# Paired weight jobs of a one-core decoder layer: the weight sums move to SBUF-to-SBUF transfers, more slots for raw weights

## The chip, the cores and the metric

The kernel runs on one core of a Trainium2 chip. The time is what the device takes for one execution, in microseconds (us). Three runs of the kernel before gave 1238.41, 1242.54 and 1246.62 us; the median, 1242.54, is its time.

## The reference

One decoder layer for a prompt of 512 tokens and a sample group of 8 x 4 tokens, 544 columns in all, d_model 1024, in float32:

```
x = x + 0.5 * SwiGLU_1(RMSNorm(x))                  # d_ff 2816
z = RMSNorm(x) @ w_in                               # 28 column blocks of 128
x = x + concat(MoBA(q_a, k_a, v_a), gate * norm(HGRN2(q_b, f_b, i_b))) @ w_out
x = x + 0.5 * SwiGLU_2(RMSNorm(x))
swiglu(x) = (silu(x @ w_gate) * (x @ w_up)) @ w_down
```

MoBA is a block-sparse attention with 8 heads of 64 (the sample group reads a paged cache of 1024 tokens through a page table), HGRN2 a gated linear recurrence with 4 heads of 128. Outputs are both groups' activations, the new keys and values and the recurrent states.

## The kernel before, in words

**Number format.** Every product of weights and activations is done in three float32r matmuls. A weight tile is split into a high part (ScalarE copies it to float32r) and a low part (VectorE subtracts the high part from the raw tile); so are activations. `products` (L667) then adds hi*hi, hi*lo and lo*hi into PSUM, 272 columns (half of 544) at a time.

**Units and jobs.** A weight unit is a raw tile of 128 rows by up to 4 blocks of 128 columns and its two parts (`split_unit`, L593). `weight_jobs` (L502) lists the jobs in the order of use. A plain job has two units for one column block. A paired job computes a 2 x 2 arrangement of blocks with seven products instead of eight (a Strassen-Winograd form): seven units, made of the quarters a11, a12, a21, a22 and of sums of them. For gate and up it takes one feature block f of both matrices, with units of 4 blocks (256 KB each) and 7 x 4 x 3 = 84 matmuls, where the two plain jobs have 96. For down it takes two output blocks, with 192 KB or 128 KB units. In each FFN the feature blocks 0 to `NREG` - 1 are plain, the others and all of down are paired. The 22 feature blocks go in groups of 6, 6, 4 and 6; after each group comes its part of down.

**Loading and splitting.** `w_load` (L575) issues one raw block per call: a plain load on SP's queue and, where the entry names a second source, an accumulating transfer of it from HBM on POOL's queue. A paired job loads five blocks, (a21 + a22), (a11 + a21), a11, a12, a22. `w_split` (L600) begins a paired job when all five have been issued; at unit 0 VectorE makes two more sums into separate tiles S0 and S1, and all seven units follow. `room` (L544) hands out slots: 6 raw and 4 split-unit slots, and in stretches of the FFNs more of both, made from tiles that are free there (`more_slots`, L560). `w_pump` (L631) splits up to `AHEAD` = 4 units ahead and loads as long as there are raw slots.

**Factors.** A paired job also needs the activations in paired form. `right_factors` (L720) makes them for gate and up in 4 sets of 18 steps on VectorE and ScalarE, spaced by `PACE`; `raw_hidden` and `hidden_paired` make the hidden ones for down.

**Order.** Nothing is scheduled on the chip. A planner (`Order`) runs through the whole program as coroutines, a backbone of matmuls and side chains, with a price for every instruction and transfer (`Engine.call`, `Order.dma` at L360), and sorts each stretch by the modelled start. The five engines then execute their queues in that order; an instruction that waits holds up all that stand behind it on its engine. All instructions are recorded at one line (L286), so the trace tells them apart by tile names: `raw`, `S`, `whi`, `wlo` for weights, `xw` for factors, `hw` for hidden factors, `xh`, `xl` for activations, which also serve as extra raw and split-unit slots, `mm` and `sm` for PSUM. `small` (L962) loads small constants and builds a table of relative biases through DRAM (`rbias`, then `rprompt` and `rsample`) during the first FFN. In the mixer (`project`, `mix`) the 28 input projections are plain jobs, between attention, recurrence and gathers of the cache that POOL issues.

Of the kernel before, what the change touches and what calls it, by code (L numbers as in the profile page):

```python
# [21 lines left out]
KD = D // 128  # L22
# [30 lines left out]
NREG = 6  # L53
AHEAD = 4
PACE = 0.8
# [124 lines left out]
class Engine:  # L180
# [75 lines left out]
class Order:  # L256
# [158 lines left out]
class Factors:  # L415
# [4 lines left out]
    def __init__(self, build, home, raw):  # L420
        self.nc = build.nc
        self.t = [build.tl(home(i)[0], [128, 2, HT], home(i)[1], F32R) for i in range(7)]
        self.u = [build.tl(raw[0], [128, 2, HT], t) for t in raw[1:]]
# [39 lines left out]
class Build:  # L463
# [38 lines left out]
    def weight_jobs(self):  # L502
# [14 lines left out]
        def plain(m, nk, r0, c0):  # L517
            job(None, [(q,) for q in quarters(m, nk, r0, c0)], nk)

        def paired(kind, nk, a11, a12, a21, a22):  # L520
            job(kind, [(a21, a22), (a11, a21), (a11,), (a12,), (a22,)], nk)
# [17 lines left out]
        for m in range(KD):  # L539
            plain(a["w_out"][0], KD, 0, 128 * m)  # L540
# [34 lines left out]
    def w_load(self):  # L575
# [10 lines left out]
        for more in src[1:]:  # L586
            self.nc.gpsimd.dma_start(raw_k, more, accum_op=ALU.add)
# [5 lines left out]
    def split_unit(self, src, nk, x):  # L593
        nc = self.nc
        hi, lo = self.take_slot(x, (F32R, F32R))
        nc.scalar.copy(hi[:, :nk], src[:, :nk])
        nc.vector.tensor_tensor(lo[:, :nk], src[:, :nk], hi[:, :nk].bitcast(F32), op=ALU.subtract)
        return hi, lo, x

    def w_split(self):  # L600
# [4 lines left out]
        if len(job["raw"]) <= (4 if job["paired"] else n) or (job["paired"] and len(self.xw) < KD // 2):  # L605
            return False
        x = self.room("w", job)
        if x is None:
            return False
        nk = job["nk"]  # L610
# [109 lines left out]
    def right_factors(self, pool, x, gain):  # L720
# [5 lines left out]
        for k in range(n):  # L726
            f = Factors(self, lambda i: (pool, f"xw{7 * k + i}"), (pool, "S0", "S1"))
# [4 lines left out]
            for step in steps + f.first() + f.right() + f.left():  # L732
                step()
# [80 lines left out]
    def raw_hidden(self, i, hs):  # L814
# [3 lines left out]
        if not odd:  # L818
            hs.append(Factors(self, lambda k: self.hidden_home(7 * p + k), (self.sums, "U0", "U1")))
# [142 lines left out]
    def small(self, rp):  # L962

        nc, a = self.nc, self.a
        loads = []

# [4 lines left out]
        self.lmi = rp.tile([128, 5, 16], I32, name="lmi")  # L971
# [21 lines left out]
        self.tab = rp.tile([33, HEADS], F32, name="tab")  # L993
# [929 lines left out]
```

## Time and profile before

| | |
|---|---|
| median of 3 runs | 1242.54 us (1238.41 to 1246.62) |
| the profiled execution | 1247.47 us, span 1245.7 us |
| TensorE / VectorE / ScalarE / POOL busy | 94% / 79% / 50% / 23% of the span |
| mean granted TensorE clock | 0.982 |
| read from HBM | 176.41 MB |
| first FFN, mixer with w_out, second FFN (about) | 17 to 437, 437 to 866, 866 to 1241 us |

Busy times are unions of the instructions' records; matmuls are pipelined, so a single record (about 290 ns) is longer than the distance between two of them. PE is TensorE, PEld its weight load, DVE VectorE, ACT ScalarE, POOL GpSimd, SP the engine that only issues transfers. In the timeline the bracket gives the idle time just before an instruction and what ended it.

### The profile page before, as it was taken

To read this page: it belongs to the slowest core of one execution; us is meant where nothing else is said; L and a number is where in the kernel's file an instruction comes from. 1 tells how busy PE (TensorE), PEld (TensorE's weight loads), DVE (VectorE), ACT (ScalarE), POOL (GpSimd) and SP (SyncE) were. 2 spreads that over 40 slices of the span, in tenths; PEclk is the share of its full clock that TensorE was granted. 3 is DMA by queue.
4 is the path that set the end of the run, shared out by engine and by line. 5 is a ranking of instruction groups with operands and counts; after the bars stand their busy time and mean duration, and the time that the engine had idled before them with its cause. 6 is when DMAs were issued, how large, how long until landed. Compare 5 with 4: busy or idle time off the path is not lost.

```text
span 1245.7 us, 27096 instructions
## 1 busy us (share of the span) xinstructions
PE 1172.4 (94%) x10339; PEld 1096.8 (88%) x10339; DVE 989.0 (79%) x2220; ACT 625.8 (50%) x1345; POOL 289.8 (23%) x271
## 2 busy tenths in 40 slices
PE   9998798999898899999999999899999899998998
PEld 8997797999898898888888877699998899998998
DVE  5998687989787869888768557657987799898896
ACT  5444554465464534555555533344443665555653
POOL 3012212222212240000133333330022222222220
PEclk9999899999998998999999999899999999999999
DMA  6248768885976572322456677452258778959764
GB/s 182 67 96 171 163 129 201 180 164 122 189 147 127 151 227 81 93 81 86 144 155 212 205 233 231 164 157 77 86 129 173 156 151 169 198 106 207 159 141 104
DMA packets 303102, 187.27 MB, mean 150 GB/s; under 512 B 15717, under 2 KB 290972, under 8 KB 302972
## 3 DMA queue, kind: packets, MB, share of 16 engines
q1 hardware_dynamic: 235100, 120.76, 34.2%
q0 software_dynamic: 67776, 64.64, 27.5%
q8 instruction: 81, 1.33, 0.4%
q14 instruction: 49, 0.40, 0.1%
q10 hardware_dynamic: 96, 0.14, 0.0%
HBM read 176.41 MB, written 11.83 MB: 151 GB/s over the span
## 4 chain that ended last, share of the span: by engine, by line
PE 46%; DVE 13%; ACT 3%; issue 2%; DMA 2%; DVEq 0%; POOL 0%; ACTq 0%; POOLq 0%; SPq 0%
PE mm L286 25%; PE sm L286 21%; DVE wlo L286 2%; DVE xl L286 2%; DVE U L286 1%; DVE S L286 1%; DMA raw<-ffn_gate 1%; DVE y L286 1%; DVE sc L286 1%; ACT xl L286 1%; DMA raw<-ffn_up 1%; DVE st L286 1%; ACT xh L286 0%; DVE ms_qk L286 0%; ACT sq L286 0%
## 5 line engine op out<-in xcount | busy, mean ns | idle before, releaser
L286 PE MATMUL mm<-xh,whi 128*128 128x272 f32 x997 | 299.7, 302 | 2.3 <-DVE y L286 2.3
L286 PE MATMUL mm<-xl,whi 128*128 128x272 f32 x998 | 289.0, 291 | 5.3 <-DVE xl L286 4.5
L286 PE MATMUL mm<-xh,wlo 128*128 128x272 f32 x966 | 280.8, 291 | 2.3 <-DVE wlo L286 2.3
L286 ACT CAST whi<-raw 128x512 fp32r<-128x512 f32 (+2 forms) x233 | 134.8, 583 | 147.3 <-PE mm L286 74.0
L286 PEld LDWEIGHTS mm<-xh,whi 128*128 128x128 f32 x997 | 189.4, 190 | 18.3 <-issue 16.9
L286 PEld LDWEIGHTS mm<-xl,whi 128*128 128x128 f32 x998 | 189.8, 190 | 7.7 <-DVE xl L286 6.1
L286 PEld LDWEIGHTS mm<-xh,wlo 128*128 128x128 f32 x966 | 183.9, 190 | 2.9 <-DVE wlo L286 2.8
L286 DVE TENSOR_TENSOR wlo<-raw,whi 128x512 fp32r<-128x512 f32 (+2 forms) x233 | 153.1, 671 | 24.4 <-ACT whi L286 23.6
L286 POOL DMA_DIRECT2D raw<-ffn_down x51 | 64.5, 1286 | 314.2 <-DVE S L286 62.1
L286 PE MATMUL mm<-xw,xh 128*128 128x272 f32 x544 | 103.6, 289 | 2.9 <-DVE U L286 2.9
L286 PE MATMUL sm<-xw,xh 128*128 128x272 f32 x512 | 98.2, 290 | 4.1 <-ACT t_g L286 3.5
L286 PEld LDWEIGHTS mm<-xw,xh 128*128 128x128 f32 x544 | 85.1, 188 | 4.1 <-DVE U L286 3.6
L286 POOL DMA_DIRECT2D raw<-ffn_up x38 | 48.7, 1315 | 159.6 <-DVE U L286 25.3
L286 PEld LDWEIGHTS sm<-xw,xh 128*128 128x128 f32 x512 | 81.2, 191 | 5.1 <-ACT t_g L286 3.7
L286 PE MATMUL mm<-xw,xl 128*128 128x272 f32 x272 | 78.7, 289 | 0.4 <-DVE xl L286 0.2
L286 PE MATMUL sm<-xw,xl 128*128 128x272 f32 x256 | 74.4, 291 | 1.7 <-DVE xl L286 1.7
L286 PE MATMUL sm<-xw,whi 128*128 128x272 f32 x384 | 73.2, 289 | 0.0
L286 PE MATMUL mm<-xw,whi 128*128 128x272 f32 x352 | 68.8, 293 | 0.9 <-DVE U L286 0.9
L286 ACT CAST xh<-raw 128x512 fp32r<-128x512 f32 (+2 forms) x94 | 52.4, 561 | 32.7 <-DMA raw<-ffn_up 18.5
L286 PEld LDWEIGHTS sm<-xw,whi 128*128 128x128 f32 x384 | 60.1, 188 | 0.7 <-issue 0.6
L286 PEld LDWEIGHTS mm<-xw,whi 128*128 128x128 f32 x352 | 56.4, 192 | 2.2 <-DVE U L286 1.4
L286 POOL DMA_INDIRECT KV<-cache_k,idx x32 | 32.8, 1025 | 104.6 <-PE sm L286 63.3
(365 smaller groups left out, 2985.0 us busy)
## 6 DMA issues: line engine op xcount, KB each, us to landing
raw<-ffn_gate SPq DMA_DIRECT2D x90, 256.0 KB
raw<-ffn_down SPq DMA_DIRECT2D x91, 192.0 KB
raw<-ffn_up SPq DMA_DIRECT2D x60, 256.0 KB
raw<-w_in SPq DMA_DIRECT2D x56, 256.0 KB
raw<-ffn_up POOLq DMA_DIRECT2D x38, 256.0 KB
raw<-ffn_down POOLq DMA_DIRECT2D x39, 192.0 KB
xl<-ffn_up POOLq DMA_DIRECT2D x20, 256.0 KB
xh<-ffn_up SPq DMA_DIRECT2D x16, 256.0 KB
```

Source lines behind the costliest of these rows:

```text
L286: call(*map(real, args), **{k: real(v) for k, v in kw.items()})
```

## The change

A paired job's five blocks become a11, (a21 + a11), a22, (a21 + a22), a12, and the added operand is the raw tile that already lies in SBUF. VectorE's two sums go in place, into a11 at unit 1 and into a12 at unit 5. Unit 0 may be split as soon as the first block is issued, units 1 and 2 after the fourth, the rest after the fifth. The low part of a22, made at unit 1 and kept for unit 6, and the low part of the second unit of every plain job but w_out's, no longer come from VectorE: ScalarE writes the negated tile in float32r and an accumulating transfer on POOL's queue adds the raw tile. `NREG` goes from 6 to 5. Raw slots beyond the 6 go from 4 to 10 in the gate/up stretches and from 4 to 12 in the first FFN's last down stretch, split-unit slots from 4 + 6 to 5 + 3 and from 4 + 8 to 5 + 4. The factors use other raw tiles, alternating, and are made two steps at a time every 1.1 us. The planner's prices of transfers change. The first projection of the mixer does both column halves at once. The small constants share a tile of another pool.

```diff
-NREG = 6
+NREG = 5
-PACE = 0.8
+PACE = 1.1
...
+                pool = self.part == "pool"
                 s = self.order.dma(self.part, 4 * args[1].shape[0] * self.free(args[1]), names,
-                                   1.0 if self.part == "pool" else 0.06)
+                                   1.3 if pool else 0.06, 2.5 if "accum_op" in kw else 2.0)
...
-    def dma(self, part, size, names, cost=0.06):
+    def dma(self, part, size, names, cost=0.06, latency=2.0):
         s = self.fit(part, self.start(part, names), cost)
-        e = self.fit("dma", s + cost + 1.5, size / 330e3) + size / 330e3
+        e = self.fit("dma", s + cost + latency, size / 280e3) + size / 280e3
...
         def paired(kind, nk, a11, a12, a21, a22):
-            job(kind, [(a21, a22), (a11, a21), (a11,), (a12,), (a22,)], nk)
+            job(kind, [(a11,), (a21, 0), (a22,), (a21, 2), (a12,)], nk)
...
         self.nc.sync.dma_start(raw_k, src[0])
-        for more in src[1:]:
-            self.nc.gpsimd.dma_start(raw_k, more, accum_op=ALU.add)
+        for n in src[1:]:
+            self.nc.gpsimd.dma_start(raw_k, job["raw"][n][0][:, :job["nk"]], accum_op=ALU.add)
...
-    def split_unit(self, src, nk, x):
+    def split_unit(self, src, nk, x, transfer=False):
+
         nc = self.nc
         hi, lo = self.take_slot(x, (F32R, F32R))
         nc.scalar.copy(hi[:, :nk], src[:, :nk])
+        if transfer:
+            nc.scalar.activation(lo[:, :nk], src[:, :nk], AF.Identity, scale=-1.0)
+            nc.gpsimd.dma_start(lo[:, :nk], src[:, :nk], accum_op=ALU.add)
+            return hi, lo, x
...
-        if len(job["raw"]) <= (4 if job["paired"] else n) or (job["paired"] and len(self.xw) < KD // 2):
+        if len(job["raw"]) <= ((0, 3, 3, 4, 4, 4, 4)[n] if job["paired"] else n):
             return False
...
         if job["paired"]:
-            s1, s3, a11, a12, a22 = (r for r, _ in job["raw"])
-            if n == 0:
-                S = [self.tl(self.sums, [128, 4, 128], f"S{i}") for i in range(2)]
-                for out, p, q in ((S[0], s1, a11), (S[1], a12, S[0])):
-                    self.nc.vector.tensor_tensor(out[:, :nk], p[:, :nk], q[:, :nk], op=ALU.add)
-                job["units"] = (a11, S[0], s1, a12, s3, S[1], a22)
-            self.units.append(self.split_unit(job["units"][n], nk, x))
-            drop = {0: (2,), 2: (0,), 3: (3,), 4: (1,), 6: (4,)}.get(n, ())
+            a11, s3, a22, s1, a12 = (r for r, _ in job["raw"])
+            if n in (1, 5):
+
+                out, p = (a11, s1) if n == 1 else (a12, a11)
+                self.nc.vector.tensor_tensor(out[:, :nk], out[:, :nk], p[:, :nk], op=ALU.add)
+            src = (a11, a11, s1, a12, s3, a12, a22)[n]
+            if n < 6:
+                self.units.append(self.split_unit(src, nk, xs[0]))
+            else:
+                self.units.append(job["last"])
+                self.release(xs[0])
+            if last:
+                job["last"] = self.split_unit(a22, nk, xs[1], True)
+            drop = {1: (2,), 2: (3,), 4: (1,), 5: (0, 4)}.get(n, ())
         else:
-            self.units.append(self.split_unit(job["raw"][n][0], nk, x))
+            self.units.append(self.split_unit(job["raw"][n][0], nk, xs[0], n == 1 and job["transfer"]))
...
-            f = Factors(self, lambda i: (pool, f"xw{7 * k + i}"), (pool, "S0", "S1"))
+            f = Factors(self, lambda i: (pool, f"xw{7 * k + i}"),
+                        [self.hidden_home(14 + k % 2 * 2 + i) for i in range(2)])
...
-            for step in steps + f.first() + f.right() + f.left():
-                step()
+            steps += f.first() + f.right() + f.left()
+            for i in range(0, len(steps), 2):
+                for step in steps[i:i + 2]:
+                    step()
                 self.order.t = self.order.free["pe"] + PACE
                 yield
...
-                        self.more_slots("a", home, [f"{t}{i}" for i in range(2) for t in ("xh", "xl")],
-                                        [(f"xh{i}", f"xl{i}") for i in range(2, KD)])
+                        self.more_slots("a", home, [f"{t}{i}" for i in range(5) for t in ("xh", "xl")],
+                                        [(f"xh{i}", f"xl{i}") for i in range(5, KD)])
...
-                self.more_slots("b", wide, [f"xw{i}" for i in range(4)],
-                                [(f"xw{i}", f"xw{i + 1}") for i in range(4, 20, 2)])
+                self.more_slots("b", wide, [f"xw{i}" for i in range(12)],
+                                [(f"xw{i}", f"xw{i + 1}") for i in range(12, 20, 2)])
...
-                      "w": [{"pool": self.wp, "tags": ("whi", "wlo"), "bufs": 4, "used": 0, "freed": [], "extra": None}]}
+                      "w": [{"pool": self.wp, "tags": ("whi", "wlo"), "bufs": 5, "used": 0, "freed": [], "extra": None}]}
...
-        yield from self.gemm(self.xg, KD, evac)
+        yield from self.gemm(self.xg, KD, evac, both=self.z_used == 1)
```

## Rows read from the trace of the kernel before

**Rows 1.** The page: busy time by engine, granted clock in 40 slices, HBM traffic.
```profile
PE 1172.4 (94%) x10339; PEld 1096.8 (88%) x10339; DVE 989.0 (79%) x2220; ACT 625.8 (50%) x1345; POOL 289.8 (23%) x271
...
PEclk9999899999998998999999999899999999999999
...
HBM read 176.41 MB, written 11.83 MB: 151 GB/s over the span
```

**Rows 2.** Chain of waits, 1122 to 1152: start us, duration us, what, count.
```profile
1139.53 10.51 PE mm L286 x84
```

**Rows 3.** Stages: length, busy us (instructions) of PE, PEld, DVE, ACT, POOL; clock, transfer share, GB/s.
```profile
17.00:437.00 420.00, 380.72 (x2868) 369.47 (x2869) 343.80 (x733) 217.46 (x454) 96.61 (x75) 0.97 0.67 144
437.00:866.00 429.00, 417.80 (x4587) 360.50 (x4587) 314.42 (x792) 196.96 (x451) 108.08 (x119) 0.98 0.50 155
866.00:1241.00 375.00, 358.88 (x2811) 353.36 (x2810) 322.64 (x683) 200.62 (x424) 81.07 (x64) 1.00 0.70 147
```

**Rows 4.** Timeline of TensorE, first FFN: start us, duration us, instruction, [idle before <-releaser].
```profile
98.59 0.39 PE L286 MATMUL mm<-hw,wlo 128*128 128x272 f32 x1 [4.76 <-DVE wlo L286]
...
140.35 0.79 PE L286 MATMUL sm<-hw,whi 128*128 128x272 f32 x2 [7.24 <-DVE x L286]
...
209.91 0.52 PE L286 MATMUL sm<-xw,xh 128*128 128x272 f32 x2 [3.46 <-ACT t_g L286]
```

**Rows 5.** Timelines of VectorE, ScalarE and SP's queue ahead of those pauses.
```profile
132.87 0.69 DVE L286 TENSOR_TENSOR S<-raw,raw 128x512 f32<-128x512 f32 x1 [1.51 <-DMA raw<-ffn_up]
...
135.28 0.62 ACT L286 CAST xh<-raw 128x512 fp32r<-128x512 f32 x1 [3.89 <-DMA raw<-ffn_up]
...
208.34 0.51 ACT L286 CAST whi<-xh 128x384 fp32r<-128x384 f32 x1 [6.76 <-DMA xh<-ffn_down]
...
188.27 0.75 SPq L286 DMA_DIRECT2D rprompt<-rbias  x1
```

**Rows 6.** Chain of waits in the second FFN: its transfers.
```profile
932.34 4.62 DMA raw<-ffn_down
...
960.22 6.72 DMA raw<-ffn_up
...
970.94 6.64 DMA raw<-ffn_gate
...
1130.80 4.58 DMA raw<-ffn_gate
```

**Rows 7.** Stages, columns as in rows 3: before unit 5; steady gate/up pairs.
```profile
38.00:77.00 39.00, 36.69 (x290) 36.24 (x290) 36.19 (x80) 20.24 (x40) 0.00 (x0) 1.00 0.26 66
...
985.00:1105.00 120.00, 118.80 (x940) 117.66 (x939) 107.58 (x218) 70.39 (x151) 30.30 (x24) 1.00 0.77 158
```

**Rows 8.** Transfer queues, 250 to 275 us: packets, MB, share of 16 engines.
```profile
q0 software_dynamic: 3387, 1.68, 54.7%
q1 hardware_dynamic: 5838, 2.89, 42.0%
```

**Rows 9.** Transfer queues, 812 to 830 us: POOL's plain loads of 2176-byte rows.
```profile
q0 software_dynamic: 640, 2.23, 35.6%
```

**Rows 10.** Groups by form, whole span: xcount | busy us, mean ns | idle before.
```profile
L286 DVE TENSOR_TENSOR wlo<-raw,whi 128x512 fp32r<-128x512 f32 x164 | 116.4, 727 | 15.2 <-ACT whi L286 14.5
...
L286 ACT CAST whi<-raw 128x512 fp32r<-128x512 f32 x164 | 100.7, 618 | 117.2 <-PE mm L286 56.1 <-issue 32.0 <-PE sm L286 8.6
```

**Rows 11.** Groups on POOL, whole span: transfers issued; the third has 128 rows.
```profile
L286 POOL DMA_DIRECT2D raw<-ffn_down x51 | 64.5, 1286 | 314.2 <-DVE S L286 62.1 <-DMA pt<-page_table 52.4 <-DVE wlo L286 33.8
L286 POOL DMA_DIRECT2D raw<-ffn_up x38 | 48.7, 1315 | 159.6 <-DVE U L286 25.3 <-DVE sq L286 21.7 <-ACT whi L286 18.9
...
L286 POOL DMA_DIRECT2D y<-xs x8 | 4.3, 550 | 22.6 <-PE mm L286 22.6
```

**Rows 12.** Stage 77 to 94, instructions on S tiles: busy of DVE, ACT; clock, share, GB/s.
```profile
77.00:94.00 17.00, 8.72 (x18) 3.62 (x7) 1.00 0.53 108
```

**Rows 13.** VectorE on xw tiles, 30 to 130 us: min/median/max ns, first and last start.
```profile
L286 DVE TENSOR_TENSOR xw<-S,xw x20: 430/442/726, 43.8 to 93.1; 128x272 fp32r<-128x272 f32 x12, 128x544 fp32r<-128x544 f32 x8
```

More of the change, by code (lines that the diff above doesn't have):

```diff
@@ L422, in __init__ @@
         self.t = [build.tl(home(i)[0], [128, 2, HT], home(i)[1], F32R) for i in range(7)]
-        self.u = [build.tl(raw[0], [128, 2, HT], t) for t in raw[1:]]
+        self.u = [build.tl(pool, [128, 2, HT], t) for pool, t in raw]
     def raw(self, q):
@@ L515, in job, with plain @@
             out.append({"kind": kind, "src": src, "nk": nk // 2, "raw": [], "done": 0, "paired": kind is not None})
-        def plain(m, nk, r0, c0):
+        def plain(m, nk, r0, c0, transfer=True):
             job(None, [(q,) for q in quarters(m, nk, r0, c0)], nk)
+            out[-1]["transfer"] = transfer
         def paired(kind, nk, a11, a12, a21, a22):
-            job(kind, [(a21, a22), (a11, a21), (a11,), (a12,), (a22,)], nk)
+            job(kind, [(a11,), (a21, 0), (a22,), (a21, 2), (a12,)], nk)
         def ffn(p, last):
@@ L539, in weight_jobs @@
         for m in range(KD):
-            plain(a["w_out"][0], KD, 0, 128 * m)
+            plain(a["w_out"][0], KD, 0, 128 * m, False)
         ffn("ffn2", "a")
@@ L604, in w_split @@
         n = job["done"]
-        if len(job["raw"]) <= (4 if job["paired"] else n) or (job["paired"] and len(self.xw) < KD // 2):
+        if len(job["raw"]) <= ((0, 3, 3, 4, 4, 4, 4)[n] if job["paired"] else n):
             return False
-        x = self.room("w", job)
-        if x is None:
+        nk, last = job["nk"], job["paired"] and n == 1
+        xs = [self.room("w", job)]
+        if last and xs[0]:
+            xs.append(self.room("w", job))
+        if None in xs:
+            for x in xs[:-1]:
+                x["used"] -= 1
+                x["freed"].insert(0, -1.0)
             return False
-        nk = job["nk"]
         if job["paired"]:
-            s1, s3, a11, a12, a22 = (r for r, _ in job["raw"])
-            if n == 0:
-                S = [self.tl(self.sums, [128, 4, 128], f"S{i}") for i in range(2)]
-                for out, p, q in ((S[0], s1, a11), (S[1], a12, S[0])):
-                    self.nc.vector.tensor_tensor(out[:, :nk], p[:, :nk], q[:, :nk], op=ALU.add)
-                job["units"] = (a11, S[0], s1, a12, s3, S[1], a22)
-            self.units.append(self.split_unit(job["units"][n], nk, x))
-            drop = {0: (2,), 2: (0,), 3: (3,), 4: (1,), 6: (4,)}.get(n, ())
+            a11, s3, a22, s1, a12 = (r for r, _ in job["raw"])
[11 more added lines that the diff above has]
+            drop = {1: (2,), 2: (3,), 4: (1,), 5: (0, 4)}.get(n, ())
         else:
-            self.units.append(self.split_unit(job["raw"][n][0], nk, x))
+            self.units.append(self.split_unit(job["raw"][n][0], nk, xs[0], n == 1 and job["transfer"]))
             drop = (n,)
@@ L818, in raw_hidden @@
         if not odd:
-            hs.append(Factors(self, lambda k: self.hidden_home(7 * p + k), (self.sums, "U0", "U1")))
+            hs.append(Factors(self, lambda k: self.hidden_home(7 * p + k), [(self.sums, "U0"), (self.sums, "U1")]))
         f = hs[p]
@@ L970, in small @@
         self.lm = self.cp.tile([128, 5, 16], U8, name="lm")
-        self.lmi = rp.tile([128, 5, 16], I32, name="lmi")
+        self.lmi = rel[:, 2 * RCHUNK:2 * RCHUNK + 80].bitcast(I32).rearrange("p (l c) -> p l c", l=5)
         load(self.lmi, a["lmask"].rearrange("p (l c) -> p l c", l=5))
@@ L992, in small @@
         load(self.ic, a["iconst"])
[L993 removed]
+        self.tab = rel[:33, 2 * RCHUNK + 80:2 * RCHUNK + 80 + HEADS]
         nc.gpsimd.memset(self.tab[32:33], NEG)
         load(self.tab[:32], a["rel_bias_table"])
[L996 to L997 removed]
+        self.rel, self.oh, self.rs = rel, rel[:33, :RCHUNK], rel[:HEADS, RCHUNK:2 * RCHUNK]
         for dst, src in loads:
@@ L1027, in small_setup @@
                                            self.ic[:, q:q + 1].to_broadcast([128, DB]), op0=ALU.mult, op1=ALU.add)
-        rd = self.dp.tile([HEADS, RLEN], F32, name="rbias")
+        rd, rel = self.dp.tile([HEADS, RLEN], F32, name="rbias"), self.rel
         for c0 in range(0, RLEN, RCHUNK):
-            oh = self.oh()
+            oh = self.oh
             nc.sync.dma_start(oh, self.a["onehot"][:, c0:c0 + RCHUNK])
             self.order.t = self.order.free["pe"] + 6.0
+            self.order.arrival(rel)
             yield
@@ L1154, in ffn1 @@
         nc = self.nc
-        with self.pool("ffn1") as pool, self.pool("relb") as rp, ExitStack() as stack:
+        with self.pool("ffn1") as pool, ExitStack() as stack:
             x = [pool.tile([128, T], F32, name=f"x{k}") for k in range(KD)]
@@ L1160, in ffn1 @@
             self.R = None
-            self.order.spawn(self.small(rp))
+            self.order.spawn(self.small())
             out = []
```

7 lines of the change are left out of this document (3 added, 4 removed).

## The prediction

> **What bounds the kernel now.** I read the whole page first. TensorE is busy for 94% of the span and its granted clock is below full in a few slices only [rows 1], so a gain has to come from the places where TensorE stands still, or from fewer matmuls. The steady price of one matmul is in the chain of waits: 84 of them in 10.51 us, 125.1 ns each, which is one paired gate/up job [rows 2]. Against that price the table by stage shows where time is lost [rows 3]. The first FFN (17 to 437 us) has 2868 matmuls, worth 358.8 us, in 420 us: 61 us lost. The second FFN (866 to 1241) has 2811, worth 351.7, in 375: 23 us lost. The mixer between them holds short and slow forms, so this division says nothing there; its TensorE is busy for 418 of 429 us and I treat it as bound by TensorE. The clock share of 0.97 in the first FFN takes up to 13 of its 61 us; that loss follows pauses, so it goes where they go.
>
> The timeline of TensorE shows the pauses: 4.76, 7.24 and 3.46 us in the first FFN, each said to wait for VectorE or ScalarE [rows 4]. One step further back it is the weights. Before the 7.24 us pause, VectorE stood 1.51 us in front of the first weight sum until an accumulating load of ffn_up had landed, and ScalarE then 3.89 us for the next one; before the 3.46 us pause ScalarE stood 6.76 us for ffn_down, behind the big bias copy (rprompt) that SP issued at 188.27 [rows 5]. In the second FFN the chain of waits names the loads themselves: 4.62, 6.72, 6.64 and 4.58 us [rows 6]. Because both sums stand ahead of all other VectorE work of their pair, one late load also holds up the evacuations behind it. The 4.76 us pause is different: VectorE is 93% busy from 38 to 77 us (36.19 of 39) [rows 7] and simply late.
>
> **The change, part by part.** *Matmuls.* With one more unit paired in each FFN, 96 matmuls become 84, twice: 24 x 0.125 = 3.0 us less. This is on the path.
>
> *Weight traffic.* A pair read seven blocks from HBM, two of them accumulating; now five plain loads, two accumulations SBUF to SBUF and a third for one low part. The rate of each kind comes from a window that holds both: the plain queue moved 2.89 MB in 42.0% of 25 us, 275 GB/s; the accumulating one 1.68 MB in 54.7%, 123 GB/s [rows 8]. A 256 KB block (262,144 B) so takes 0.95 us of all engines plain and 2.13 us accumulating. Before: 5 x 0.95 + 2 x 2.13 = 9.0 us of the 10.51 us that TensorE needs, 86%. After: 4.77 + 3p, where p is the price of one accumulation in rows of 2 KB rather than 512 B, which the trace does not hold. Upper end: the rate per byte stays, p = 2.13, sum 11.2 (106%). Lower end: the surplus is per packet. It is 64.6 - 28.8 = 35.8 ns (share x 25 us x 16 engines over the packet counts of rows 8); long rows move at 348 GB/s (2.23 MB in 35.6% of 18 us) [rows 9], so p = 0.75 + 128 x 0.0358 / 16 = 1.04, sum 7.9 (75%). I take p = 1.5, twice the plain price of a long row, since an accumulation reads its destination as well: 9.3 us, 88%. By itself this gives nothing back: the load on the transfer engines stays where it was. The Trainium skill (DMA: Bandwidth & Descriptors, section Where 436 GB/s comes from) holds that SBUF to SBUF transfers are bound by a fabric of 435 GB/s; estimated from that, p would be 0.6 us and the sum 6.6. No run here shows such a transfer, and the accumulating rows are far below that rate, so I keep 1.5.
>
> *Latency.* A sum is now a chain: load, then accumulation. Under load the chain of waits has 4.6 us for a plain load and 6.7 for an accumulating one [rows 6], together 11.3 us, more than one pair (10.5). It stays hidden only if a pair is loaded more than one pair ahead. Raw slots go from 10 to 16 in the gate/up stretch, at five blocks per pair from 2.0 to 3.2 pairs ahead, so it is hidden there; in the first FFN's last down stretch from 10 to 18. If that cover fails, each pair can show 11.3 - 10.5 = 0.8 us. The Trainium skill (the same page, Anatomy of one DMA — SWDGE (gpsimd) path) fits 2.0 us plus the bytes over 436 GB/s, an estimated 2.6 us per accumulation; the trace disagrees by 2.5 times because the engines are shared here.
>
> *Head of the queue.* A pair's first split needs one block instead of five, and the sums move to units 1 and 5. A late accumulation then stops VectorE in front of unit 1, with at least one unit (12 matmuls, 1.5 us) more in hand. A late last block no longer stops anything before unit 3.
>
> *Engines.* Each gate/up pair drops one VectorE subtraction (0.727 us) and gains one ScalarE pass (0.618 us) [rows 10]. In the steady gate/up stretch VectorE is busy for 107.6 of 120 us, ScalarE for 70.4 [rows 7]; VectorE goes from 90% to about 83%, ScalarE from 59% to 65%. TensorE already runs at its steady price there (940 x 0.125 = 117.6 of 120), so this buys slack, not time. POOL issues three transfers instead of two, but of 128 rows: the row for 128-row transfers says 0.55 us, the 512-row ones 1.3 [rows 11]; 1.7 us per pair instead of 2.6. Behind an accumulation that waits for its two loads stand on POOL's queue the next accumulations and low parts, and in the mixer the gathers. The 28 low parts in the mixer cost VectorE 20 us less (28 x 0.727) of 314 busy us, where it is not the bound: 0, with +-5 for POOL's order around the gathers. SP issues five plain loads per pair before and after, only earlier: nothing.
>
> *The earlier pair.* The paired input factors must now be ready when unit 5 starts, at about 77 us, not at the first pair after the down stretch. After 77 us VectorE still spends 8.7 us on them [rows 12], and the last subtraction lies at 93.1 [rows 13]. Found before 77: 2.8 us of slack [rows 7] and up to 6 plain low parts moved to transfers, 4.4 us, at a DMA share of 0.26. Missing: 1.5 us, between 0 and 8.7. I take +2. The faster pace of the factors (two steps per 1.1 us) makes this possible and crowds the evacuations.
>
> *The rest.* The planner's new transfer prices only reorder the queues; the first projection run with both halves at once saves under 1 us. Both 0, within the range.
>
> **Sum.** First FFN: the 7.24 us and 3.46 us pauses go with deeper loading, with half of the clock loss (6) and a tenth of the other 37 us (4): -21. Second FFN: of 23 us the DMA-led third: -8. Matmuls -3, unit 5 +2, mixer 0: -30. The profiled execution took 1247.47 us (span 1245.7), so 1217; the median of the runs is 4.9 us under it, which gives 1213, and I say 1214. The likeliest case alone: 1184 to 1232.
>
> **Rivals.** (a) *Accumulations cost by the byte* (slower). It also covers the case that the transfers are cut into 512 B rows after all, so that the change does not do what it says. From p = 1.91 us on (4.77 + 3p = 10.51) the transfer engines set the pace of every pair. At 2.13 each of the 34 gate/up pairs loses 0.65 us, the 24 down pairs with 192 KB blocks 0.49 and the 8 with 128 KB 0.33 (three quarters and half of it): 37 us on the median, less 3 for matmuls: 1277; between 1.91 and there 1255 to 1277. For it: rows 8, where length has no say in the rate seen; against it: long plain rows do move faster [rows 9]. Chance 0.18.
> (b) *The waits only change their name.* Loading is deeper, but a pair's accumulation comes late by the 0.8 us above in some of the 66 pairs and VectorE, still above 80%, hands it on; with unit 5 late by 8.7 us: -30 + 7 + 18 (the 0.8 us in a third of the pairs) on the median of 1242.5: 1237; in two thirds, 1255. For it: POOL stands idle before its transfers for 314 us before ffn_down ones [rows 11], so its queue is led by waits. The Trainium skill (SBUF — State Buffer, section SBUF: two separate sides) warns that VectorE work through the shared port keeps POOL from writing descriptors, which would add to this case. In the trace 38 issues of 512 rows, beside a VectorE that is up to 90% busy, took 1.3 us on average [rows 11], so this adds nothing to the chance. Chance 0.21.
> (c) *Nearly all pauses go*, p near 1.04: -61 -23 plus a remainder of 15: 1170 to 1184. Chance 0.07.
> Forecast: 0.54.
>
> **How the numbers follow.** One per cent is 12.4 us, about what the spread of the runs can tell from no change. Faster (under 1230): (c) and nearly all of the forecast, 0.60. Slower (over 1255): (a), 0.18. Within: (b) and the edge of the forecast, 0.22. The range leaves out most of (c) and of (a): 1182 to 1256.
>
> **What will show it.** Right: 24 matmuls fewer; HBM reads down by about 28 MB from 176 [rows 1] (two blocks less in 32 gate/up and 32 down pairs, 16.8 + 11.5 MB); POOL's transfers near 0.55 us; accumulating rows of 1.5 to 2 KB; VectorE's share in the gate/up stretch lower by some 6 points; no TensorE pause above 3 us in the first FFN's paired stretches, and its clock share above 0.98. Wrong: an accumulating queue still near 123 GB/s with the transfer share at 1.0 through the pairs (a); new waits on accumulated blocks in VectorE's first sum, or a pause of 5 us or more at unit 5 (b).

## The result, and the profile after

The changed kernel takes 1229.22 us (median of four runs, 1226.89 to 1231.29) against 1242.0 for the kernel before on the same chip (four runs): ratio 0.9895 [0.9857, 0.9933]. A repeat on another chip gave 1228.14, ratio 0.986 [0.9828, 0.9892]. Both intervals lie below 1, so it is faster, by 12.8 to 17.6 us (1.0 to 1.4%) where 28.5 were forecast: direction and range held, the size was about half.

From the page of the changed kernel, the lines that answer to [rows 1]:

```profile
PE 1168.5 (95%) x10315; PEld 1095.0 (89%) x10315; DVE 940.2 (77%) x2118; ACT 686.1 (56%) x1471; POOL 341.2 (28%) x387
...
PEclk8999999999999899999999999999998999999999
...
HBM read 148.62 MB, written 11.83 MB: 131 GB/s over the span
```

There are 24 matmuls fewer and 27.8 MB fewer are read, as forecast. The table by stage, with the columns of [rows 3, 7]; the first three rows are the stages, the fourth the stretch before unit 5, the last the steady gate/up pairs:

```profile
17.00:426.00 409.00, 378.60 (x2857) 367.40 (x2856) 331.77 (x695) 242.66 (x507) 111.24 (x121) 0.97 0.76 174
426.00:856.00 430.00, 416.84 (x4585) 360.70 (x4584) 294.09 (x764) 210.80 (x480) 135.26 (x148) 0.98 0.61 173
856.00:1224.00 368.00, 359.48 (x2804) 354.00 (x2803) 306.31 (x647) 222.60 (x472) 92.31 (x106) 0.99 0.78 176
38.00:77.00 39.00, 36.44 (x279) 36.22 (x278) 35.13 (x80) 24.70 (x47) 6.02 (x7) 0.96 0.48 101
975.00:1095.00 120.00, 119.15 (x944) 118.23 (x943) 102.01 (x207) 77.81 (x165) 33.01 (x38) 1.00 0.81 183
```

The first FFN is 11 us shorter, the second 7, the mixer between them as long as before. In the steady pairs VectorE fell from 90% to 85% and ScalarE rose from 59% to 65%, while TensorE had nothing left to win there. The transfer share *rose* from 0.77 to 0.81: the load did not get lighter.

The transfer queues of the changed kernel, 250 to 275 us, as in [rows 8] (packets, MB, share):

```profile
q0 software_dynamic: 1237, 1.98, 46.3%
q1 hardware_dynamic: 4070, 1.99, 28.3%
```

1.98 MB in 46.3% of 25 us are 171 GB/s, so 256 KB take 1.53 us. The mean packet is 1.6 KB.

What is left of TensorE's pauses, from its timeline (columns as in [rows 4]): the three longest in the two FFNs.

```profile
55.47 0.39 PE L287 MATMUL mm<-xh,wlo 128*128 128x272 f32 x1 [2.56 <-DVE wlo L287]
...
104.39 0.82 PE L287 MATMUL sm<-hw,whi 128*128 128x272 f32 x2 [3.91 <-ACT whi L287]
...
923.50 0.60 PE L287 MATMUL mm<-xl,whi 128*128 128x272 f32 x1 [3.17 <-ACT whi L287]
```

Of the three pauses of [rows 4] the second and third are gone but for 1.03 us at 136.57; the first is 0.85 us shorter and stands seven matmuls later, at 104.39. The one at 923.50 lies at the same place in the second FFN, the first down stretch. The chain of waits in the second FFN, which held four transfers with 22.6 us [rows 6], holds two:

```profile
913.13 4.23 DMA raw<-ffn_down
918.52 3.58 DMA xh<-raw
```

For the pause at 104.39 POOL's timeline shows the same chain of a load and an accumulation:

```profile
95.22 0.86 POOL L287 DMA_DIRECT2D raw<-raw  x1 [13.28 <-DMA raw<-ffn_down]
95.75 2.10 POOL L287 DMA_DIRECT2D xl<-xh  x2
96.83 1.91 POOL L287 DMA_DIRECT2D xh<-raw  x1
```

The accumulation at the head of POOL's queue waited for its own loads of ffn_down, and six other transfers left in one burst behind it. On SP's queue ten loads of ffn_down into newly opened extra slots (xl and xh, from 84.35 us on) stand ahead of the next raw block:

```profile
89.92 0.44 SPq L287 DMA_DIRECT2D xh<-ffn_down  x1
90.53 0.37 SPq L287 DMA_DIRECT2D raw<-ffn_down  x1
```

The transfer share is 0.92 from 85 to 99 us and 1.16 in the pause, so the deeper loading that opens there is likely part of the delay itself; no run separates it. After the pause the granted clock (third column from the right) is 0.78, so part of that stretch ran at the lower level (1.2 GHz). It falls behind shorter pauses too: from 398 to 404 us, around a pause of 1.58 us.

```profile
104.40:112.00 7.60, 7.60 (x48) 7.50 (x49) 6.87 (x16) 4.30 (x10) 2.61 (x3) 0.78 0.77 165
398.00:404.00 6.00, 4.60 (x23) 4.16 (x24) 5.39 (x13) 2.01 (x5) 0.82 (x1) 0.77 0.83 225
```

The following table puts the profiled execution of each run on one scale. It counts matmuls of 272 columns and takes the start of the last one of a stage; each column is the length of a stage in us (the first from the span's start). A row is one execution, not a median: that of experiment 11 (slack -0.05) lies 9.1 us above its kernel's median, those of 5 and 8 lie 4.6 and 4.3 below, that of the kernel before 5.5 above. "Slack" is a constant of the planner that is explained at experiments 10 to 12.

```
kernel                    slack  first FFN  mixer, w_out  second FFN
before                    -0.10    436.3       417.8        385.7
before                    -0.15    436.5       422.5        386.5
before, new prices        -0.10    423.3       429.8        383.2
after                     -0.10    425.5       419.1        377.7
after                     -0.15    419.0       414.5        377.7
after                     -0.05    426.8       421.4        378.8
after, old prices   -0.10/-0.15  442.5/446.2  419.9/421.9  389.8/388.6
after, old slots    -0.10/-0.15  428.4/433.8  419.1/423.6  384.6/385.7
after, no low parts -0.10/-0.15  421.8/424.3  417.1/415.5  385.0/386.2
after, sums HBM    -0.10/-0.15  439.8/449.1  419.3/424.7  385.0/387.3
after, NREG 6       -0.10/-0.15  429.3/430.2  424.1/419.1  391.6/394.0
after, light start -0.10/-0.15  417.5/423.2  423.0/422.2  378.3/378.1
after, true prices        -0.10    434.3       429.7        378.1
```

The column to read first is the last one. With all five parts that were tested in it (prices, slots, low parts, sums, `NREG`), the second FFN takes 377.7 to 378.8 us whatever else is varied; with any one of them taken out, 384.6 or more. The other two columns move by up to 9 us between rows that differ in nothing but the order, some of it from one execution to the next.

### The profile page after: what moved, and what is told of

Read it like the earlier page. It is cut to its first block, busy times and chain, and to the rows that moved or that the text cites. A ratio compares the mean times of both kernels' runs of the same rounds, so it can differ in the third digit from the quotient of the medians.

```text
span 1228.2 us, 27296 instructions
## 1 busy us (share of the span) xinstructions
PE 1168.5 (95%) x10315; PEld 1095.0 (89%) x10315; DVE 940.2 (77%) x2118; ACT 686.1 (56%) x1471; POOL 341.2 (28%) x387
## 5 line engine op out<-in xcount | busy, mean ns | idle before, releaser
L287 POOL DMA_DIRECT2D wlo<-raw x70 | 69.5, 999 | 241.8 <-ACT wlo L287 158.3
L287 PE MATMUL sm<-xw,whi 128*128 128x272 f32 x552 | 106.5, 289 | 0.0
L287 PE MATMUL mm<-xw,whi 128*128 128x272 f32 x552 | 106.3, 289 | 0.0
L287 DVE TENSOR_TENSOR wlo<-raw,whi 128x512 fp32r<-128x512 f32 (+2 forms) x144 | 96.4, 674 | 9.6 <-ACT whi L287 8.6
L287 PEld LDWEIGHTS sm<-xw,whi 128*128 128x128 f32 x552 | 86.8, 189 | 1.1 <-issue 1.1
L287 PEld LDWEIGHTS mm<-xw,whi 128*128 128x128 f32 x552 | 87.4, 190 | 0.0
L287 PE MATMUL mm<-xw,wlo 128*128 128x272 f32 x276 | 79.9, 290 | 1.4 <-DVE wlo L287 1.4
L287 PE MATMUL sm<-xw,wlo 128*128 128x272 f32 x276 | 79.7, 289 | 0.4 <-DVE wlo L287 0.4
L287 DVE TENSOR_TENSOR xl<-raw,xh 128x512 fp32r<-128x512 f32 (+2 forms) x97 | 58.0, 598 | 9.2 <-ACT xh L287 5.9
L287 ACT CAST whi<-xl 128x512 fp32r<-128x512 f32 (+2 forms) x80 | 44.2, 557 | 29.2 <-DVE xl L287 13.6
```

Of the source, the lines that this page charges most:

```text
L287: call(*map(real, args), **{k: real(v) for k, v in kw.items()})
```

## The experiments

Ratios are to the kernel before, run on the same chip in turn. Unless said otherwise the diff is against the changed kernel. The first nine have the planner's slack as it was, the last nine vary the order and repeat what mattered in another one.

**1, 14. The planner's prices of before.**

```diff
-1.3 if pool else 0.06, 2.5 if "accum_op" in kw else 2.0)
+1.0 if pool else 0.06, 1.5)
-        e = ... size / 280e3
+        e = ... size / 330e3
```

> The kernel after, with the planner's transfer prices of before (latency 1.5 us, 330 KB per us, 1.0 us on POOL); everything else as after. Theory A (the first 5.7 us are lost because the new prices make the planner split the second weight job later and put VectorE subtractions ahead of activations that the matmuls wait for): the 480th 272-column matmul comes back from 86.9 us to about 83, and in the paired stretches some of it is given away again because the planner expects blocks too early; total 1226 to 1234 against 1229. Theory B (the loss is the factors for the earlier pair crowding VectorE): the 480th matmul stays at 86 to 87.

Measured 1259.93 us, 1.013 [1.0081, 1.0178]: slower than the kernel before. Neither theory had a loss of this size. The start does not come back (plain jobs 0 to 4 end at 87.66 us). TensorE's waits over the whole span (total us, times, longest), the rows that concern low parts:

```profile
PE mm L287 <- DMA wlo<-xl: 5.5, 3, 3.2
PE sm L287 <- DMA wlo<-xh: 4.9, 3, 2.3
...
PE mm L287 <- DMA wlo<-xh: 4.2, 2, 2.4
PE sm L287 <- DMA wlo<-xl: 3.5, 1, 3.5
```

TensorE waits directly for low parts made by transfer, 18.1 us in 9 waits. The changed kernel has no such row among its first eleven. That a planner that thinks an accumulation lands early puts the matmuls that need it too early fits this; the edit changes the price of plain loads as well, and the two were not separated.

> The kernel after with SLACK at -0.15 and the planner's transfer prices of before. Theory A (the prices are a cause: without them TensorE waits for low parts by transfer, seen as waits of PE on wlo from DMA): 15 us or more above 1219, with such waits in the trace. Theory B (the 31 us of the first try were an unlucky order): within 8 us of 1219.

Measured 1263.41, 1.0122 [1.0076, 1.0167], with 19.1 us of the same waits. It holds in the second order too.

**2, 15. The extra slots of before** (raw 4 instead of 10, in the last down stretch 4 instead of 12; the tiles that this frees become split-unit slots again, 6 instead of 3 and 8 instead of 4).

```diff
-... [f"{t}{i}" for i in range(5) for t in ("xh", "xl")] ...
+... [f"{t}{i}" for i in range(2) for t in ("xh", "xl")] ...
-... [f"xw{i}" for i in range(12)] ...
+... [f"xw{i}" for i in range(4)] ...
```

> The kernel after, with the extra slots of before (4 raw and 6 split-unit ones in the gate/up stretches, 4 and 8 in the last down stretch). Theory A (deeper loading is what took the pauses away): most of the gain goes, 1238 to 1245. Theory B (the relief of VectorE and the sums by transfer did it): 1229 to 1232.

Measured 1240.36, 0.9963 [0.9939, 0.9988]: most of the gain is gone. Two pauses of TensorE that the changed kernel lacks, one in each FFN, and ScalarE ahead of the first of them:

```profile
216.79 0.60 PE L287 MATMUL sm<-hw,xh 128*128 128x272 f32 x1 [8.61 <-ACT xh L287]
...
1130.25 0.52 PE L287 MATMUL mm<-xw,xh 128*128 128x272 f32 x2 [2.53 <-ACT xh L287]
```

```profile
212.39 0.51 ACT L287 CAST xh<-xl 128x384 fp32r<-128x384 f32 x1 [5.88 <-DMA xl<-ffn_down]
```

The timeline of TensorE names ScalarE; one step further back it is again a block of ffn_down that came late, the same kind of pause as at 209.91 [rows 4, 5].

> The kernel after with SLACK at -0.15 and the extra slots of before. Theory A (deeper loading is a cause): 8 us or more above 1219, one long pause again near 210 us where the bias copy goes out. Theory B: within 8 us of 1219.

Measured 1249.0, 0.9999 [0.9977, 1.0022]: a pause of 9.17 us at 220.91, and the second FFN again 8.0 us longer. The deeper raw slots are needed in either order, since the split-unit slots that come in their place do not make up for them.

**3, 18. All low parts by VectorE.**

```diff
-        if transfer:
+        if False:
             nc.scalar.activation(lo[:, :nk], ...
```

> The kernel after, with every low part made by VectorE as before (no negated copy on ScalarE, no third accumulation). Theory A (slots): 1226 to 1232, since the transfer load falls by 1.5 us of 9.3 per pair and VectorE had slack. Theory B (relief of VectorE): 1236 to 1243, VectorE back at about 90% in the gate/up stretch.

Measured 1231.7, 0.9898 [0.9857, 0.9939], the same as the changed kernel over the whole. By stage it is not the same: the second FFN loses 7.3 us, while the first is 3.7 us and the mixer 2.0 shorter in this execution. The plain jobs of the second FFN and then its unit 5 (columns as above), in this kernel with two of its pauses, and in the changed one:

```profile
838.80:906.50 67.70, 64.74 (x502) 63.86 (x501) 59.93 (x134) 32.95 (x61) 1.80 (x2) 0.97 0.30 81
906.50:920.30 13.80, 11.53 (x86) 11.31 (x85) 7.41 (x16) 5.74 (x15) 4.70 (x6) 0.94 0.96 237
```

```profile
873.72 0.40 PE L287 MATMUL mm<-xh,wlo 128*128 128x272 f32 x1 [1.83 <-DVE wlo L287]
...
918.10 0.52 PE L287 MATMUL sm<-xw,whi 128*128 128x272 f32 x2 [2.27 <-DVE U L287]
```

```profile
844.60:908.40 63.80, 62.90 (x503) 62.24 (x502) 54.27 (x124) 37.75 (x71) 10.36 (x12) 1.00 0.61 133
908.40:918.90 10.50, 10.50 (x86) 10.50 (x85) 5.97 (x13) 5.13 (x13) 0.91 (x2) 1.00 0.90 264
```

The same 502 matmuls take 67.7 us instead of 63.8, and unit 5 takes 13.8 instead of 10.5. That is where low parts by transfer help, not in the steady pairs. The busy share of VectorE alone does not explain it: 89% here (59.93 of 67.7), 85% in the changed kernel, but 91% without a loss in the kernel before (56.63 of 62.40 us from 854.1 to 916.5, where unit 5 is not a pair). So the transfers pay back what the rest of the change puts there; against the kernel before, these jobs win nothing.

> The kernel after with SLACK at -0.15 and all low parts made by VectorE. Theory A (the low parts by transfer give nothing, as VectorE had slack): within 6 us of 1219. Theory B (they give, and the first try's 2 us were the order's): 8 us or more above.

Measured 1231.06, 0.9895 [0.9867, 0.9922]: 12 us above the changed kernel in the same order (experiment 10), 8.5 of them in the second FFN. That is theory B: the low parts by transfer are worth something, and the 2 us of the first order hid it. What the rest comes from is open.

**4, 16. The sums' second operand from HBM again**, in 512 B rows.

```diff
-            self.nc.gpsimd.dma_start(raw_k, job["raw"][n][0][:, :job["nk"]], accum_op=ALU.add)
+            self.nc.gpsimd.dma_start(raw_k, job["src"][n][0], accum_op=ALU.add)
```

> The kernel after, with the second operand of each sum read from HBM in 512-byte rows again; order and slots as after. Transfer load per gate/up pair 4.77 + 2 x 2.13 + 1.5 = 10.5 us, as long as TensorE needs. If the load of the transfer engines matters at that depth: 1240 to 1255. If only slots or VectorE matter: 1229 to 1233.

Measured 1251.46, 1.0061 [1.0038, 1.0084]. The transfer queues of this kernel, 960 to 1020 us, and the pause that it has in the last stretch:

```profile
q0 software_dynamic: 7521, 4.62, 57.0%
q1 hardware_dynamic: 15412, 7.64, 45.2%
```

```profile
1148.43 0.52 PE L287 MATMUL mm<-xw,xh 128*128 128x272 f32 x2 [3.75 <-ACT sq L287]
```

57.0% and 45.2% are more than the engines' whole time. In this window TensorE still keeps up (59.79 of 60 us busy). The pause names ScalarE; one step further back VectorE stood for an accumulating load that POOL had issued at 1138.38:

```profile
1146.75 0.69 DVE L287 TENSOR_TENSOR xl<-xl,xh 128x512 f32<-128x512 f32 x1 [3.45 <-DMA xh<-ffn_up]
```

This makes the load of rival (a), without its pace: the steady pairs do not slow down, the time goes in pauses elsewhere.

> The kernel after with SLACK at -0.15 and the second operand of each sum read from HBM in 512-byte rows. Theory A (the transfer engines are as busy as TensorE then: 10.5 us per pair): 15 us or more above 1219, most of it in the paired stretches. Theory B: within 8 us of 1219.

Measured 1267.49, 1.0145 [1.0103, 1.0187], with a pause of 8.78 us at 241.78.

**5, 13. A lighter start.** In the first plain jobs the call that pumps splits and loads only loads.

```diff
                 if n == 4 and m == 0:
-                    self.w_pump()
+                    while self.w_load():
+                        pass
```

> The kernel after, but in the start the weights are only loaded ahead, not split ahead (after has a fifth split-unit slot, so one more unit is split between the first activations). Theory A (that unit's VectorE subtraction stands in front of an activation that TensorE waits for and costs 3 of the 5.7 us lost in the first 81): the 48th to 72nd matmul come back by 2 to 3 us, total 1225 to 1228. Theory B (the loss is run to run or in the factors' pace): no change at the 72nd matmul, 1229.

Measured 1231.07, 0.9852 [0.9804, 0.9899]. The plain jobs 0 to 4 end at 82.49 us instead of 86.78 (before: 81.10), so 4.3 of 5.7 us come back there (1.1 of them before the first matmul, which starts at 10.42 instead of 11.55), and the first FFN takes 417.5 instead of 425.5. The mixer then takes 423.0 instead of 419.1, and the total hardly moves. (This execution is 4.6 us faster than the median of its kernel, so part of the 8.0 us is its own.) VectorE in the start of the kernel before, of the changed one, and of this one:

```profile
14.22 1.28 DVE L286 TENSOR_TENSOR wlo<-raw,whi 128x512 fp32r<-128x512 f32 x2
...
20.32 3.09 DVE L286 SCALAR_TENSOR_TENSOR xl<-x,gains,xh 128x544 fp32r<-128x544 f32 x2
```

```profile
14.34 0.69 DVE L287 TENSOR_TENSOR wlo<-raw,whi 128x512 fp32r<-128x512 f32 x1
...
17.93 1.84 DVE L287 TENSOR_TENSOR wlo<-raw,whi 128x512 fp32r<-128x512 f32 x1
...
20.30 3.08 DVE L287 SCALAR_TENSOR_TENSOR xl<-x,gains,xh 128x544 fp32r<-128x544 f32 x2
23.30 1.84 DVE L287 TENSOR_TENSOR wlo<-raw,whi 128x512 fp32r<-128x512 f32 x1
25.07 1.85 DVE L287 SCALAR_TENSOR_TENSOR xl<-x,gains,xh 128x544 fp32r<-128x544 f32 x1
```

```profile
16.82 1.85 DVE L287 TENSOR_TENSOR wlo<-raw,whi 128x512 fp32r<-128x512 f32 x1
18.59 0.68 DVE L287 COPY x<-sm 128x512 f32<-128x512 f32 x1
19.19 4.87 DVE L287 SCALAR_TENSOR_TENSOR xl<-x,gains,xh 128x544 fp32r<-128x544 f32 x3
```

With the fifth split-unit slot the pump splits one unit more, and its low part stands at 23.30 ahead of the last activation. That one's low part ends at 23.4 us in the kernel before, at 26.9 in the changed one and at 24.1 in this one. The edit takes away all splitting at this point, not the fifth slot alone. In all other runs of the changed kernel and its variants these jobs end at 84.3 to 89.4 us.

> The kernel after with SLACK at -0.15 and, in the start, weights only loaded ahead, not split. The start's 4.3 us came back in the run with SLACK -0.1. Theory A (the start's loss is a place of its own): the 480th 272-column matmul at about 82 instead of 86, total 1213 to 1217, faster than both kernels. Theory B (what the start gives is lost in the reordering behind it): 1217 to 1223.

Measured 1230.13, 0.9852 [0.9811, 0.9892], a miss: no faster than the changed kernel in the same order but behind it by 0.6% (0.9791 there, experiment 10). The start ends early again (83.39 us instead of 86.04), but two pauses of TensorE follow:

```profile
100.93 0.82 PE L287 MATMUL sm<-hw,whi 128*128 128x272 f32 x2 [5.17 <-ACT whi L287]
...
216.34 0.82 PE L287 MATMUL sm<-hw,xh 128*128 128x272 f32 x2 [4.48 <-DVE x L287]
```

**6. The kernel before with the new prices** (diff against the kernel before).

```diff
-        e = ... s + cost + 1.5, size / 330e3
+        e = ... s + cost + latency, size / 280e3    # latency and cost as in the change
```

> The kernel before, with the planner's new transfer prices alone. Theory A (the prices are a cause of their own: a planner that knows how late blocks come keeps VectorE and ScalarE from standing in front of them): 1230 to 1238 against 1243. Theory B (the prices only matter for the low parts by transfer, on which TensorE waits directly): 1239 to 1247.

Measured 1247.09, 0.9992 [0.9965, 1.0019]. No difference in all, but a large one inside: 13.0 us less in the first FFN, 2.5 in the second, 12.0 more in the mixer.

**7. True prices**: the planner is told the rate at which accumulations were measured.

```diff
-        e = ... size / 280e3
+        e = ... size / rate    # 175e3 for accumulating transfers, else 280e3
```

> The kernel after, with accumulating transfers priced at 175 KB per us in the planner (1.5 us per 256 KB, what their packets took) instead of 280. Theory A (the closer the planner's prices, the fewer waits): 1220 to 1227. Theory B (the price after is already late enough and a longer one makes the planner put real pauses into its order): 1229 to 1240.

Measured 1250.24, 1.0002 [0.9981, 1.0023]: worse, and by more than theory B had. The second FFN stays at 378.1, the first has a pause of 8.43 us at 248.10, the mixer takes 429.7. A truer rate is not a better order (the latency of 2.5 us stayed).

**8, 17. `NREG` back to 6.**

```diff
-NREG = 5
+NREG = 6
```

> The kernel after, with six plain feature blocks as before. By the matmuls alone it is 3.0 us slower, 1232. Theory A (the factors for the earlier pair crowd VectorE in the first 81 us): the 480th matmul comes 1 to 3 us earlier and the total is 1228 to 1231. Theory B (they do not): 1232 to 1236.

Measured 1257.17, 1.0067 [1.0043, 1.009], far above both theories (1228 to 1236). The plain jobs 0 to 4 end at 85.35 us, 1.4 earlier. TensorE's pauses in the first down stretch of either FFN, and ScalarE ahead of the first:

```profile
114.51 0.82 PE L287 MATMUL sm<-hw,whi 128*128 128x272 f32 x2 [6.09 <-ACT whi L287]
...
946.29 0.59 PE L287 MATMUL sm<-xl,whi 128*128 128x272 f32 x1 [6.05 <-ACT whi L287]
```

```profile
107.46 0.51 ACT L287 CAST whi<-raw 128x384 fp32r<-128x384 f32 x1 [3.38 <-DMA raw<-ffn_down]
...
109.69 0.51 ACT L287 CAST whi<-raw 128x384 fp32r<-128x384 f32 x1 [1.29 <-DMA raw<-ffn_down]
```

The extra slots open where the first paired gate/up job begins. With `NREG` 6 that is after the first down stretch, which must do with 6 raw slots for pairs of five blocks; with 5 it is before it. That this is the cause is read from the code and the places of the pauses; `NREG` 6 with the slots opened earlier wasn't tried.

> The kernel after with SLACK at -0.15 and six plain feature blocks. By the matmuls alone 3.0 us above 1219. Theory A (the sixth paired block is a cause of the 21 us of the first try): 15 us or more above. Theory B (that loss was the order's): 1217 to 1228.

Measured 1247.63, 1.0033 [1.0015, 1.005], the same pauses (7.85 at 115.34, 5.69 at 941.75).

**9. The changed kernel again.**

> The kernel after, unchanged, beside the others on the same chip. Every theory: 0.985 to 0.993 of the kernel before.

Measured 1228.14, 0.986 [0.9828, 0.9892], as quoted above; the profile agrees with the first to 0.2 us.

**10, 11, 12. A neutral reorder.** The planner takes a side chain's step when its model has it ready within the slack of TensorE's time. Another slack changes the order alone.

```diff
-SLACK = -0.1
+SLACK = -0.15    # 10; -0.05 in 11; -0.15 in the kernel before in 12
```

> The kernel after, with the planner's tie-break SLACK at -0.15 us instead of -0.1: no work, transfer or price changes, only which chain the planner steps first, so the queues come out in another order. Theory A (the pauses that went, went because of deeper loading and right prices): within 5 us of after. Theory B (the order that came out of the constants of after is a lucky one, and its gain over before is of the size of what any reordering does): 8 to 20 us slower than after.

Measured 1219.21 (1218.18 to 1220.22), 0.9791 [0.9758, 0.9824], the fastest of all: 8.9 us faster than experiment 9, where theory A had 5 at most and theory B a loss.

> As the run before, with SLACK at -0.05 us. Theory A: within 5 us of after. Theory B: 8 to 20 us slower than after.

Measured 1225.55, 0.9835 [0.9801, 0.9868].

> The kernel before with SLACK at -0.15 us: the same neutral reordering of the kernel before. Theory A: within 5 us of before. Theory B: 5 to 20 us slower or faster than before, as its constants had been found with it.

Measured 1253.87, 1.0061 [1.0041, 1.0081]. These three and experiment 9 ran on one chip beside the kernel before (1245.77): the order alone is worth -8.9 us (10) to the changed kernel and +8.1 to the kernel before; the -2.6 of experiment 11 lie within its scatter (1223.48 to 1234.61). At the slack as it was the change brings 17.6 us there, at -0.15 it brings 1253.87 - 1219.21 = 34.7. The changed kernel's order was not a lucky one: one other is faster, the second no slower.

## Why the prediction was right in sign and wrong in size

The sum, term by term, from the table by stage and the ends of the plain jobs and unit 5 within it (us, at the last matmul):

```
                                       forecast  measured
plain jobs 0 to 4 of the first FFN         0       +5.7
unit 5, with its 12 matmuls fewer        +0.5      +0.1
first FFN after unit 5                    -21     -16.6
mixer and w_out                            0       +1.3
second FFN, with 12 matmuls fewer        -9.5      -7.9
sum                                       -30     -17.4
```

These are the two profiled executions, and that of the kernel before is 5.5 us above its median: by the medians it is 12.8, and 17.6 on the second chip.

*The steps that failed* lie in the first FFN. The plain jobs before unit 5 stood at 0, without a reason given: no step priced what the fifth split-unit slot puts ahead of the first activations. They cost 5.7 us, and without the splitting there 4.3 come back (5), 2.7 in the other order (13). `NREG` back to 6 gives 1.4 and 1.6 (8, 17), so the earlier pair's factors may be the rest; the factors' pace alone wasn't tried. After unit 5, the -21 held 10.7 for two pauses, 4 for the rest and 6 for half of the clock loss. This stretch in both kernels, the same 2284 matmuls:

```profile
93.60:436.60 343.00, 306.53 (x2284) 296.01 (x2284) 276.46 (x587) 178.39 (x379) 84.60 (x66) 0.96 0.75 159
99.40:425.80 326.40, 303.84 (x2284) 294.03 (x2283) 263.65 (x554) 195.26 (x414) 88.82 (x99) 0.97 0.80 185
```

TensorE's idle time fell from 36.5 to 22.6 us, 13.9 where 14.7 were forecast. Its busy time fell by 2.7 where the clock was to give 6. "That loss follows pauses, so it goes where they go" is the step: the pauses that went were long, and the shorter ones that stayed or came take the clock down as well (0.78 behind 3.91 us, 0.77 around 1.58). Part of the 13.9 was luck: the prediction's list lacks a pause of 4.46 us in the last down stretch of the kernel before, of which 1.47 are left at the same matmul.

```profile
397.25 0.59 PE L286 MATMUL mm<-hw,whi 128*128 128x272 f32 x1 [4.46 <-ACT hw L286]
...
383.06 0.39 PE L287 MATMUL sm<-hw,whi 128*128 128x272 f32 x1 [1.47 <-ACT hw L287]
```

*Weight traffic* was right: p was taken as 1.5 us and is 1.53, so a pair costs 4.77 + 3 x 1.53 = 9.4 us of the transfer engines, 89% of its TensorE time. The Trainium skill's fabric rate (DMA: Bandwidth & Descriptors, section Where 436 GB/s comes from), from which 0.6 us was estimated, does not price an accumulating transfer here: it runs at 171 GB/s. Rival (a) hung on this price. With the short rows back (4, 16) the kernel is slower than before, so the load matters; that it sets the pace of every pair, as (a) had it, did not show: the steady pairs ran at full pace with the engines full. Two slips of the working changed nothing here: at p = 1.91 (a) loses nothing per pair, so its lower end is 1240 and not 1255; and the packets behind the 348 GB/s of [rows 9] were 3.5 KB on average (2.23 MB in 640), not the 2176-byte rows named there, so the lower end of p leaned on longer rows than the accumulations have.

*Latency and depth* were right: without the slots the late blocks are back (2, 15). But the prediction counted pairs only in the gate/up stretches and the last down stretch. In the first down stretch POOL's queue is led by a wait of 13.28 us, and a pause of 3.91 us takes the place of the old one of 4.76, which the forecast had left standing; with 7.6 us at clock 0.78 behind it, 3.91 + 0.22 x 7.6 = 5.6 us stay there. That is rival (b) at one place. That no pause would exceed 3 us and that the clock share would pass 0.98 was wrong (0.97 as before).

*Engines* said that relief of VectorE buys slack, not time. That holds for the steady pairs, and fails in the plain jobs and at unit 5, where VectorE's low parts are waited for: 7.3 and 8.5 us in the second FFN (3, 18). The +2 for unit 5 was right in size: 1.6 beside the matmuls (12.3 us for 84, where 96 took 12.2).

*The rest* failed as well, though in the kernel's favour, so that it does not account for the missing half. "The planner's new transfer prices only reorder the queues ... Both 0": they are worth 2.4 to 3.3% to the changed kernel (the ratios of 1 and 14 against 0.9895 or 0.986 and 0.9791), and alone they take 15.5 us from the FFNs of the kernel before while they give 12.0 to its mixer (6). An order that is written out ahead is part of the machine that the price has to fit; where the transfers change, the prices belong to the mechanism.

*Matmuls* sized `NREG` by 3 us. It also moves the place where the extra slots open, and `NREG` as a whole is worth 1.7 to 2.4% (8, 17, reckoned in the same way).

In the second FFN each of five parts, taken out alone, costs 7 to 16 us, and all together bring 7.9 (8.8 at slack -0.15). So the parts do not add: each removes a wait that would stand in for the others, and a sum of single terms could give the direction but not the size. And the totals scatter by order: of the 11.2 us between the changed kernel and experiment 10, 6.5 lie in the first FFN, 4.6 in the mixer and none in the second FFN. The forecast of 1214 lies 5 us below experiment 10 and 15 below the changed kernel. A point estimate for the whole could hardly have been better than that scatter, and that the total fell inside the range is in part luck.

Open are the 12 us of experiment 18 as far as they lie outside the second FFN, and why the lighter start is worth 8.0 us in the first FFN in one order and costs 4.2 in another. The first projection with both halves and the new tile of the small constants weren't tried alone.

## What to carry to other kernels

In a kernel whose order is planned ahead, a new kind of transfer needs its price in the planner as much as its place in the code, and the scatter of a neutral reorder should be measured before any single edit is judged by the total. When the waits lead back to late blocks, ask from which point on the deeper buffers are open, not only how many there are. Judge an edit in the stage that is least disturbed by the order: here the second FFN stayed within 1.1 us with all five parts in it and lost 6.9 or more without one, while the total of experiment 3 showed no loss.

## What the runs showed of the hardware that was not expected

Accumulating transfers from SBUF to SBUF, in rows of 1 and 2 KB (1.6 KB on average), ran at 171 GB/s where plain loads ran at 281 (1.99 MB in 28.3% of 25 us); accumulating from HBM in 512 B rows, 123 [rows 8]. Source and row length changed together, so which of them gave the gain is not shown.

POOL's record of one accumulation of 128 rows is 0.86 us when it stands alone, not 0.55 as for the plain ones of [rows 11]; in a burst the next one starts 0.53 us later (95.22, 95.75), so the pitch, not the record, is what POOL's queue pays. In the steady pairs POOL's busy time rose from 30.30 us [rows 7] to 33.01, where a third less per pair was forecast.

VectorE's low part takes 0.69 us at 14.34 and 1.84 at 17.93 and 23.30, when POOL adds squares (1.41 to 1.48 us each) at the same time; the copy out of PSUM beside the same work stays at 0.68. The Trainium skill (SBUF — State Buffer, section SBUF: two separate sides) describes an exclusive lock between a VectorE operation with two SBUF inputs and a POOL operation that reads SBUF, and these rows agree with it.
